# A decoder layer on one core: u and hT moved off the 512-byte grid, a third input buffer in the first block, a late h, a norm taken by tokens, and a last block stored in three pieces

## The chip, the cores and the metric

The kernel runs on one core of a Trainium2 chip. Its time is what the device takes for one launch, in microseconds; the median of three runs is 1830.02 us (1829.93 to 1830.12). The profile is one further execution of the same program. The engines are named as in the profile: PE is TensorE (matmuls; PEld are its weight loads), DVE is VectorE, ACT is ScalarE, POOL is GpSimd, SP is the engine that issues most transfers. "Queue" with SP, ACT or POOL means transfers issued by that engine.

## What is computed

One layer on 256 tokens of width 2048, all in float32:

```python
h = x + 0.5 * swiglu(rms_norm(x, g1), w_gate1, w_up1, w_down1)     # 2048 -> 5632 -> 2048
u = rms_norm(h, g_mix)
proj = u @ w_in                       # forgetting attention: q, k, v, gates; window attention: q, k, v
o = concat(rms_norm(fox(...)), rms_norm(window(...)))
h = h + o @ w_out
y = h + 0.5 * swiglu(rms_norm(h, g2), w_gate2, w_up2, w_down2)

def rms_norm(x, g): return x * rsqrt(mean(x * x, axis=-1) + 1e-6) * g
def swiglu(x, wg, wu, wd): return (silu(x @ wg) * (x @ wu)) @ wd
```

## The kernel before

Each weight is read from HBM once, in pieces of 128 rows by 1024 columns of float32 (512 KB; two tiles of K by 512 columns). Every operand of a large matmul is split into a rounded part and the rest (`hi` and `lo`), and a product is three matmuls: hi by hi (L187), hi by lo (L188), lo by hi (L189). The activations are the stationary operand, loaded 128 x 128 at a time; the weights stream past, 512 columns a time (388 in one projection of the mixer).

`weights` (L90 to L102) fetches a piece on SP's queue into `raw`, rounds it on ACT into `whi` (L100) and takes the rest on DVE into `wlo` (L101); there are four buffers of each. `token_major` (L192) runs over pairs of K tiles, here called groups: for each of two K tiles and for each of two halves of the tokens it issues the three matmuls, 12 a group. `split_scaled` (L158) makes the two parts of an activation: ACT scales and rounds (L160), DVE takes the rest (L161). The normed input is held in two halves, `u0` and `u1`, of eight K tiles each; they are made anew for the first feed-forward stage, for the mixer and for the second feed-forward stage, and `u0` also holds the window attention's output before its projection. The activations inside a feed-forward stage are in `hT`, 44 K tiles.

A feed-forward stage is `gate_up` (L224) with 11 blocks of 512 columns, each a gate product and an up product over u, then `down` (L281) with 4 blocks over hT. After the gate product ACT applies silu with the norm's factor (L243), after the up product DVE multiplies (L247), and PE transposes the result into hT two groups into the next block (`into_rows`, L221).

The first block of the first stage is special (`first_block`, L303): u isn't there yet. For each of eight groups it fetches 256 KB of x, transposed, into `xc` (two buffers, L306), fetches the weight in two halves, makes two K tiles of u, and has ACT square `xc` and POOL add the squares up into `ss1` (L166 to L173). After the block it fetches the constants `cst` (the identity for transposes among them), the positions and x itself by tokens into `h` (L318 to L321) on SP's queue, and `rstd_tokens` (L175) sums the squares over partitions by eight one-column matmuls (L180).

The order in which each engine takes its instructions is not that of the text: a planner lays it out ahead of time by its own estimate of durations, within what depends on what, and gives the fetches of `weights` priority. So the fetches of h stand in SP's queue ahead of some of the first block's own pieces, and the first pieces of the up product's weights too. Each engine and each queue then takes its list in order.

At the end, the last block of the second stage's `down` adds both token halves into h on DVE (L258) and stores each of them, 128 x 512, on ACT's queue (L714).

Tiles are placed one after another in each partition. Unused tiles (`pad`, `sppad`, `mpad`) fill up to a place: before, `h`, `u0`, `u1`, all of `raw`, `whi`, `wlo`, both `hT` and the attention's stationary tiles begin at multiples of 512 bytes.

Of the kernel before, what the change touches and what calls it, by code (L numbers as in the profile page):

```python
# [9 lines left out]
F32 = mybir.dt.float32  # L10
F32R = mybir.dt.float32r
I32 = mybir.dt.int32
BF16 = mybir.dt.bfloat16
AF = mybir.ActivationFunctionType
ALU = mybir.AluOpType
AX = mybir.AxisListType

P = 128
D = 2048
SEQ = 256  # L20
NT = SEQ // P
KD = D // P
FF = 5632
KF = FF // P
# [42 lines left out]
def hybrid_layer(ctx: ExitStack, tc: tile.TileContext, a: dict, out: bass.AP):  # L67
    nc = tc.nc

    keep = ctx.enter_context(tc.tile_pool(name="keep", bufs=1))  # L70
# [19 lines left out]
    def weights(src, tiles=None, at=0):  # L90

        tiles = tiles or weight_tiles()
        if src.shape[1] % 512:
            n = src.shape[1] // 2
            raw, hi, lo = (t.rearrange("p (k n) -> p k n", k=2)[:, :, :n] for t in tiles)
            src = src.rearrange("p (k n) -> p k n", k=2)
        else:
            raw, hi, lo = (t[:, at : at + src.shape[1]] for t in tiles)
        nc.sync.dma_start(raw, src)
        nc.scalar.copy(hi, raw)  # L100
        nc.vector.tensor_tensor(out=lo, in0=raw, in1=hi.bitcast(F32), op=ALU.subtract)  # L101
        return tiles[1:]  # L102


    cst = keep.tile([P, C_END], F32, name="cst")
    vec = keep.tile([P, 256], F32, name="vec")
    pos = keep.tile([P, NT], I32, name="pos")
# [3 lines left out]
    h = keep.tile([P, NT, D], F32, name="h")  # L111
# [5 lines left out]
    m_caus = m_fox[:, P:SEQ]  # L117
    nc.scalar.dma_start(vec[:, :V_END], a["vec"])

    def half_u(i):  # L120
        return keep.tile([P, 8, 2, SEQ], F32R, tag="u%d" % i, name="u%d" % i, bufs=1)

# [5 lines left out]
    def tiles_of(t):  # L128
        return lambda k: t[:, k]
# [36 lines left out]
    def add_squares(ssq, src, first):  # L166

        if first:
            nc.scalar.activation(ssq, src, AF.Square)
            return  # L170
        sq = sp.tile([P, 2, SEQ], F32, tag="sqh", name="sqh", bufs=2)
        nc.scalar.activation(sq, src, AF.Square)
        nc.gpsimd.tensor_tensor(out=ssq, in0=ssq, in1=sq, op=ALU.add)  # L173

    def rstd_tokens(ssq, width, tag):  # L175

        pb = small_ps()
        for t in range(NT):
            for i in range(2):
                nc.tensor.matmul(  # L180
                    pb[:, t : t + 1], lhsT=ssq[:, i, t * P : (t + 1) * P], rhs=ones[:, 0:1],
                    start=(i == 0), stop=(i == 1),
                )
        return mean_rsqrt(sp, pb[:, :NT], NT, width, tag)

    def mm3(o, shi, slo, mhi, mlo, start, stop):
        nc.tensor.matmul(o, lhsT=shi, rhs=mhi, start=start, stop=False)  # L187
        nc.tensor.matmul(o, lhsT=shi, rhs=mlo, start=False, stop=False)  # L188
        nc.tensor.matmul(o, lhsT=slo, rhs=mhi, start=False, stop=stop)  # L189


    def token_major(acc, u, nk, src_w, width=512, then=(), early=None):  # L192

        for kg in range(nk // 2):
            if early is not None:
                parts = early(kg)
            else:
                with tc.high_priority():
                    parts = weights(src_w[kg])
            hi, lo = parts  # L200
            for k in range(2):
                kk = kg * 2 + k
                m = slice(k * 512, k * 512 + width)
                for t in range(NT):
                    ts_ = slice(t * P, (t + 1) * P)
                    mm3(
                        acc[t][:, :width], u(kk)[:, 0, ts_], u(kk)[:, 1, ts_], hi[:, m], lo[:, m],
                        start=(kk == 0), stop=(kk == nk - 1),
                    )
            if kg == 1:  # L210
                for f in then:
                    f()
# [40 lines left out]
    def residual(c, acc, scale):  # L253

        cs = slice(c * 512, (c + 1) * 512)
        for t in range(NT):
# [2 lines left out]
                out=h[:, t, cs], in0=acc[t], scalar=sc, in1=h[:, t, cs], op0=ALU.mult, op1=ALU.add  # L259
            )  # L260

    def next_u(u, ssq, gcol, c):

        cs = slice(c * 512, (c + 1) * 512)
        for t in range(NT):
            sq = sp.tile([P, 512], F32, tag="sqh", name="sqh", bufs=2)
            nc.scalar.activation(sq, h[:, t, cs], AF.Square, accum_out=ssq[:, t, c : c + 1])

        def finish(k, v):
            for j in range(2):  # L270
                split_scaled(u(k + j), v[:, j, :], vec[:, gcol + k + j : gcol + k + j + 1])

        return lambda: into_rows(h[:, :, cs], c, finish)

    def rstd_blocks(ssq, tag):

        tot = sp.tile([P, NT], F32, tag=tag + "s", name=tag + "s")
        nc.vector.tensor_reduce(out=tot, in_=ssq, axis=AX.X, op=ALU.add)
        return mean_rsqrt(sp, tot, NT, D, tag)

    def down(hT, w, then, done):  # L281
        for c in range(D // 512):
            acc = acc_pair()
            token_major(acc, tiles_of(hT), KF, w[c], then=then)
            residual(c, acc, 0.5)
            then = done(c)
        return then


    sp = ctx.enter_context(tc.tile_pool(name="sp", bufs=1))  # L290
    sp.tile([P, 392], F32, name="sppad")
    u1 = new_u()
    ss1 = sp.tile([P, 2, SEQ], F32, tag="ss", name="ss1")
    with tc.tile_pool(name="f1", bufs=1) as fp:
        hT = fp.tile([P, KF, 2, SEQ], F32R, name="hT1")

        zero = fp.tile([P, 512], BF16, name="zero")
        nc.vector.memset(zero, 0.0)
        warm = small_ps()
        for i in range(WARM):  # L300
            nc.tensor.matmul(warm, lhsT=zero[:, 0:P], rhs=zero, start=True, stop=True)

        def first_block(g):  # L303
            def early(kg):
                xc = fp.tile([P, 2, SEQ], F32, tag="xc", name="xc", bufs=2)
                nc.sync.dma_start(xc, a["xT"][kg])  # L306
                tiles = weight_tiles()
                for i in range(2):
                    at = i * 512
                    weights(a["wg1"][0][kg][:, at : at + 512], tiles, at)  # L310
                for j in range(2):
                    k = 2 * kg + j
                    split_scaled(u1(k), xc[:, j, :], vec[:, V_G1 + k : V_G1 + k + 1])
                add_squares(ss1, xc, kg == 0)
                return tiles[1:]

            token_major(g, u1, KD, None, early=early)
            nc.sync.dma_start(cst, a["cst"])  # L318
            nc.sync.dma_start(pos, a["pos"])
            for t in range(NT):  # L320
                nc.sync.dma_start(h[:, t, :], a["x"][t])  # L321
            return rstd_tokens(ss1, D, "r1")

        then = gate_up(fp, u1, None, hT, a["wg1"], a["wu1"], first_block)
        um = new_u()
        ssm = sp.tile([P, NT, 4], F32, tag="ssb", name="ssm", bufs=2)
        then = down(hT, a["wd1"], then, lambda c: [next_u(um, ssm, V_GM, c)])
    rm = rstd_blocks(ssm, "rm")


    with tc.tile_pool(name="mix", bufs=1) as mp:
        ap_ = mp
# [35 lines left out]
        for i, q in ((0, Q1B), (1, Q2B)):  # L368
            nc.vector.scalar_tensor_tensor(
                out=red, in0=cnt[:, i, :], scalar=q, in1=red, op0=ALU.mult, op1=ALU.add  # L370
# [5 lines left out]
            out=part[:, 1, :], in0=red, scalar=-1.0, in1=red, op0=ALU.mult, op1=ALU.max  # L376
        )
        nc.vector.tensor_scalar(
            out=part[:, 1, :], in0=part[:, 1, :], scalar1=-1.0, scalar2=float(np.pi / 2), op0=ALU.mult, op1=ALU.add
# [82 lines left out]
        for c in range(4):  # L462
            acc = acc_pair()
            token_major(acc, um, KD, a["ws"][c], SWC, then=then)
            then = []
# [3 lines left out]
        def fox_mm(hf, i):  # L469
# [11 lines left out]
            out=z, in0=prs[:, :, 0:NH], in1=vec[:, V_BF : V_BF + NH].unsqueeze(1).broadcast_to([P, NT, NH]), op=ALU.add  # L481
# [16 lines left out]
        for t in range(NT):  # L498
            for aa in range(2):
                n = nqk // 2  # L500
                sq = ap_.tile([P, n * HD], F32, tag="sq", name="sq")
                nc.scalar.activation(sq, prs[:, t, NH + aa * n * HD : NH + (aa + 1) * n * HD], AF.Square)
                nc.vector.tensor_reduce(
                    out=ssw[:, t, aa * n : (aa + 1) * n], in_=sq.rearrange("p (j e) -> p j e", e=HD),
# [3 lines left out]
        rw = rw.rearrange("p (t j) -> p t j", t=NT)  # L508
        nc.vector.tensor_scalar_mul(rw[:, :, 0:NH], rw[:, :, 0:NH], HD**-0.5)

        ap_.tile([P, 96], F32, name="mpad")

        def unit_tile(shape, dt, name):
            return ap_.tile(shape, dt, tag="aT", name=name, bufs=3)
# [5 lines left out]
        for t in range(NT):  # L520
# [18 lines left out]
            ts_ = slice(t * P, (t + 1) * P)  # L539
            for aa in range(2):  # L540
                qp = ap_.tile([P, 5, P], F32, tag="qp", name="qp", bufs=2)
                for dst, j0, n in ((qp[:, 0:4, :], aa * 8, 8), (qp[:, 4:5, :], NH + 2 * aa, 2)):
                    nc.vector.tensor_tensor(
                        out=dst.rearrange("p g (b e) -> p b g e", b=2),
                        in0=qr[:, j0 : j0 + n, :].rearrange("p (b g) e -> p b g e", b=2),
# [151 lines left out]
        then = []  # L697
        for c in range(D // 512):
            project(0, c, oTf, rx, then)
            then = [next_u(u2, ss2, V_G2, c)]  # L700
# [3 lines left out]

    rm2 = rstd_blocks(ss2, "rm")
    with tc.tile_pool(name="f2", bufs=1) as fp:
        hT = fp.tile([P, KF, 2, SEQ], F32R, name="hT2")
        then = gate_up(fp, u2, rm2, hT, a["wg2"], a["wu2"])
        y = out.rearrange("(t p) d -> p t d", p=P)

        def store(c):
            cs = slice(c * 512, (c + 1) * 512)
            for t in range(NT):
                nc.scalar.dma_start(y[:, t, cs], h[:, t, cs])  # L714
            return []

        down(hT, a["wd2"], then, store)

# [69 lines left out]
```

## Time and profile before

| what | us |
|---|---|
| median of three runs (lowest, highest) | 1830.02 (1829.93, 1830.12) |
| the profiled execution's own time | 1831.65 |
| its span, first to last event | 1829.5 |
| PE busy | 1818.0 |
| DVE busy | 984.1 |
| ACT busy | 844.9 |
| POOL busy | 21.3 |
| first large matmul starts | 5.89 |
| last matmul starts | 1824.95 |

The page also says that 336 MB are read from HBM, 185 GB/s over the span, and that the granted clock of PE is full in every one of its 40 slices. In the rows of groups, the columns are line, engine and operation, output and inputs by name, shapes, count, then busy us, mean ns of one, and the idle time of the engine before them with what ended it. In timelines a row is start, duration, engine, line, operation. In windows the columns are start and end, length, then busy us and count of each engine, granted clock, busy share of the DMA engines, GB/s. A matmul's duration runs from its start to its modelled end; the next one starts long before that, so the pace of PE is the distance of starts.

### The profile page before, as it was taken

What the parts mean: (1) busy time and instruction counts of PE and PEld (TensorE: products, weight loads), DVE (VectorE), ACT (ScalarE), POOL (GpSimd) and SP (SyncE); (2) the same over time, 40 slices, a digit from 0 to 9 for tenths busy, and PEclk for the clock granted to TensorE, in tenths of its full rate; (3) what the DMA queues carried; (4) which work ended last, traced back from release to release, by engine and by line L of the source; (5) the groups of instructions that cost most, each with busy time, mean ns of one, the idle gap of its engine ahead of it and who ended that gap; (6) DMA issues with size and microseconds to landing.
All of it is one profiled execution on the core that took longest, in us unless ns stands there. A gap on an engine that the chain in (4) does not pass through costs nothing.

```text
span 1829.5 us, 21808 instructions
## 1 busy us (share of the span) xinstructions
PE 1818.0 (99%) x8396; PEld 1513.9 (83%) x8396; DVE 984.1 (54%) x1194; ACT 844.9 (46%) x1073; POOL 21.3 (1%) x27
## 2 busy tenths in 40 slices
PE   8999999999999999999999999999999999999999
PEld 6888888888888888998888788888888888888887
DVE  6545454545544544668766665454554545444443
ACT  6444444444434434554767554444444444433332
POOL 2000000000000000000000000000000000000000
PEclk9999999999999999999999999999999999999999
DMA  8555555555555555564344355555555555556663
GB/s 302 194 186 194 186 194 185 194 185 195 186 193 186 192 193 187 168 209 171 125 140 142 135 175 194 186 194 185 194 186 193 184 188 192 188 193 206 207 203 119
DMA packets 100536, 339.79 MB, mean 186 GB/s; under 512 B 10832, under 2 KB 19152, under 8 KB 100176
## 3 DMA queue, kind: packets, MB, share of 16 engines
q1 hardware_dynamic: 99136, 336.19, 53.4%
q10 hardware_dynamic: 1296, 2.21, 0.4%
q8 instruction: 65, 1.06, 0.2%
q14 instruction: 39, 0.32, 0.0%
HBM read 336.27 MB, written 2.10 MB: 185 GB/s over the span
## 4 chain that ended last, share of the span: by engine, by line
PE 98%; DMA 1%; ACT 0%; DVE 0%; issue 0%; ACTq 0%; DVEq 0%
PE acc L187 31%; PE acc L189 31%; PE acc L188 31%; PE sm L221 1%; PE sm L450 1%; DMA raw<-in_wg 1%; PE sc L565 1%; PE sc L636 1%; PE sm L456 1%; DMA xc<-in_xT 0%; PE sm L617 0%; PE sm L457 0%; DMA vec<-in_vec 0%; PE sm L180 0%; PE sm L551 0%; ACT whi L100 0%
## 5 line engine op out<-in xcount | busy, mean ns | idle before, releaser
L101 DVE TENSOR_TENSOR wlo<-raw,whi 128x1024 fp32r<-128x1024 f32 (+2 forms) x648 | 777.2, 1201 | 799.1 <-ACT whi L100 798.3
L100 ACT CAST whi<-raw 128x1024 fp32r<-128x1024 f32 (+2 forms) x648 | 668.5, 1032 | 895.1 <-PE acc L189 878.7
L187 PE MATMUL acc<-whi,u 128*128 128x512 f32 (+1 forms) x1792 | 694.8, 389 | 4.1 <-ACT u L160 3.5
L188 PE MATMUL acc<-wlo,u 128*128 128x512 f32 (+1 forms) x1792 | 692.6, 387 | 0.1
L189 PE MATMUL acc<-whi,u 128*128 128x512 f32 (+1 forms) x1792 | 690.8, 387 | 0.9 <-DVE u L161 0.9
L187 PEld LDWEIGHTS acc<-whi,u 128*128 128x128 f32 x1792 | 336.8, 188 | 70.3 <-ACT u L160 4.4
L189 PEld LDWEIGHTS acc<-whi,u 128*128 128x128 f32 x1792 | 336.4, 188 | 66.5 <-DVE u L161 1.9
L188 PEld LDWEIGHTS acc<-wlo,u 128*128 128x128 f32 x1792 | 336.9, 188 | 64.7 <-DVE wlo L101 0.9
L187 PE MATMUL acc<-whi,hT 128*128 128x512 f32 x704 | 274.3, 390 | 0.0
L189 PE MATMUL acc<-whi,hT 128*128 128x512 f32 x704 | 273.9, 389 | 0.0
L188 PE MATMUL acc<-wlo,hT 128*128 128x512 f32 x704 | 273.9, 389 | 0.0
L189 PEld LDWEIGHTS acc<-whi,hT 128*128 128x128 f32 x704 | 132.2, 188 | 27.6
L188 PEld LDWEIGHTS acc<-wlo,hT 128*128 128x128 f32 x704 | 132.2, 188 | 27.2
L187 PEld LDWEIGHTS acc<-whi,hT 128*128 128x128 f32 x704 | 132.2, 188 | 27.1
L428 ACT ACTIVATE s<-s,nm 128x128 f32<-128x128 f32 (+1 forms) x64 | 28.3, 445 | 7.6 <-DVE nm L421 4.6
L230 DVE TENSOR_TENSOR hT<-sm,hT 128x512 fp32r<-128x512 f32 x44 | 28.2, 682 | 0.0
L187 PE MATMUL acc<-whi,oTf 128*128 128x512 f32 x64 | 25.2, 393 | 0.0
L188 PE MATMUL acc<-wlo,oTf 128*128 128x512 f32 x64 | 25.0, 391 | 0.0
L189 PE MATMUL acc<-whi,oTf 128*128 128x512 f32 x64 | 24.9, 389 | 0.0
L229 ACT CAST hT<-sm 128x512 fp32r<-128x512 f32 x44 | 23.5, 585 | 0.0
L221 PEld LDWEIGHTS sm<-cst,s 128*128 128x128 f32 x176 | 20.5, 140 | 2.9
L221 PE MATMUL sm<-cst,s 128*128 128x128 f32 x176 | 22.8, 272 | 0.0
(175 smaller groups left out, 563.5 us busy)
## 6 DMA issues: line engine op xcount, KB each, us to landing
raw<-in_wu SPq DMA_DIRECT2D x176, 512.0 KB, 3.2
raw<-in_wd SPq DMA_DIRECT2D x176, 512.0 KB, 3.2
raw<-in_wg SPq DMA_DIRECT2D x168, 512.0 KB, 3.2
raw<-in_wf SPq DMA_DIRECT2D x48, 512.0 KB, 3.6
raw<-in_wo SPq DMA_DIRECT2D x32, 512.0 KB, 3.5
raw<-in_ws SPq DMA_DIRECT2D x32, 388.0 KB, 3.6
raw<-in_wg SPq DMA_DIRECT2D x16, 256.0 KB, 5.3
xc<-in_xT SPq DMA_DIRECT2D x8, 256.0 KB, 4.8
```

The source lines that it names most:

```text
L100: nc.scalar.copy(hi, raw)
L101: nc.vector.tensor_tensor(out=lo, in0=raw, in1=hi.bitcast(F32), op=ALU.subtract)
L187: nc.tensor.matmul(o, lhsT=shi, rhs=mhi, start=start, stop=False)
L188: nc.tensor.matmul(o, lhsT=shi, rhs=mlo, start=False, stop=False)
L189: nc.tensor.matmul(o, lhsT=slo, rhs=mhi, start=False, stop=stop)
L221: nc.tensor.transpose(bt[:, j * SEQ + t * P : j * SEQ + (t + 1) * P], src[:, t, m], ident)
L229: nc.scalar.copy(hs[:, :, 0, :], v)
L230: nc.vector.tensor_tensor(out=hs[:, :, 1, :], in0=v, in1=hs[:, :, 0, :].bitcast(F32), op=ALU.subtract)
L428: nc.scalar.activation(s[:, j, :], s[:, j, :], AF.Exp, bias=nm[:, i, j : j + 1], accum_out=den[:, i, j : j + 1],)
L450: nc.tensor.transpose(bt[:, j * P : (j + 1) * P], src[:, j, :], ident)
L456: nc.tensor.matmul(bo[rows, c0 : c0 + SEQ], lhsT=vals(0, j), rhs=p0[:, j, :], start=True, stop=False)
L565: nc.tensor.matmul(o_, lhsT=qk[aa][:, j, blk * P : (blk + 1) * P], rhs=qk[aa][:, 4 + half, 0:nk], start=True, stop=True,)
```

## The change

Placing. Unused tiles of 256, 128 and 128 bytes are put before, between and behind `u0` and `u1`, so that `u0` begins 256 and `u1` 384 bytes past a multiple of 512; what follows (`raw`, `whi`, `wlo`) is again on multiples of 512. The filling in the pool `sp` is cut from 1568 to 192 bytes, which with the tiles that go (`ss1` as it was, three small ones of its norm) puts the first `hT` 64 bytes past a multiple of 512; a new tile of 128 bytes puts the second 192 past. `mpad` is cut by 64 bytes, so that the attention's tiles stay where they were against 512.

First block. `xc` gets three buffers. From the third group on the weight piece is fetched, rounded and subtracted whole instead of in two halves. The squares of `xc` and POOL's additions are gone. h, the constants and the positions are fetched on POOL's queue instead of SP's; each half of h first gets one column copied from the 13th K tile of u (`held`), so that its fetch waits for the seventh group, and the constants get a column copied from h, so that their fetch waits for h to have landed. The norm is taken as at the later stages: ACT squares h by blocks of 512 columns and sums them along the row (`squares`, 8 instructions with an accumulator each), DVE reduces the four sums (`rstd_blocks`). The eight one-column matmuls are gone.

End. In the last block the last group runs all six matmuls of the first token half, then all six of the second. The first half is evicted and stored whole, the second in two pieces of 256 columns; the stores go by SP's queue.

```diff
+    keep.tile([P, 64], F32, name="upad0")
+    keep.tile([P, 8, 2, SEQ], F32R, tag="u0", name="u0", bufs=1)
+    keep.tile([P, 32], F32, name="upad1")
+    keep.tile([P, 8, 2, SEQ], F32R, tag="u1", name="u1", bufs=1)
+    keep.tile([P, 32], F32, name="upad2")
...
-            for k in range(2):
+            order = [(k, t) for k in range(2) for t in range(NT)]
+            if apart and kg == nk // 2 - 1:
+                order.sort(key=lambda kt: kt[1])
+            for k, t in order:
...
+    def squares(ssq, c):
+        for t in range(NT):
+            sq = sp.tile([P, 512], F32, tag="sqh", name="sqh", bufs=2)
+            nc.scalar.activation(sq, h[:, t, c * 512 : (c + 1) * 512], AF.Square, accum_out=ssq[:, t, c : c + 1])
...
+            if last:
+                for t, a0, n in ((0, 0, 512), (1, 0, 256), (1, 256, 256)):
+                    cs = slice(c * 512 + a0, c * 512 + a0 + n)
+                    nc.vector.scalar_tensor_tensor(
+                        out=h[:, t, cs], in0=acc[t][:, a0 : a0 + n], scalar=0.5, in1=h[:, t, cs],
+                        op0=ALU.mult, op1=ALU.add,
+                    )
+                    nc.sync.dma_start(out[:, t, cs], h[:, t, cs])
+                return []
...
-    sp.tile([P, 392], F32, name="sppad")
+    sp.tile([P, 48], F32, name="sppad")
...
-                xc = fp.tile([P, 2, SEQ], F32, tag="xc", name="xc", bufs=2)
+                xc = fp.tile([P, 2, SEQ], F32, tag="xc", name="xc", bufs=3)
                 nc.sync.dma_start(xc, a["xT"][kg])
                 tiles = weight_tiles()
-                for i in range(2):
-                    at = i * 512
-                    weights(a["wg1"][0][kg][:, at : at + 512], tiles, at)
+                if kg < 2:
+                    for at in (0, 512):
+                        weights(a["wg1"][0][kg][:, at : at + 512], tiles, at)
+                else:
+                    weights(a["wg1"][0][kg], tiles)
...
-                add_squares(ss1, xc, kg == 0)
...
-            nc.sync.dma_start(cst, a["cst"])
-            nc.sync.dma_start(pos, a["pos"])
+            held = u1(12)[:, 1, 0:1].bitcast(F32)
             for t in range(NT):
-                nc.sync.dma_start(h[:, t, :], a["x"][t])
-            return rstd_tokens(ss1, D, "r1")
+                nc.vector.tensor_copy(h[:, t, 0:1], held)
+                nc.gpsimd.dma_start(h[:, t, :], a["x"][t])
+            nc.vector.tensor_copy(cst[:, 0:1], h[:, 1, 0:1])
+            nc.gpsimd.dma_start(cst, a["cst"])
+            nc.gpsimd.dma_start(pos, a["pos"])
+            ss1 = sp.tile([P, NT, 4], F32, tag="ssb", name="ss1", bufs=2)
+            for c in range(4):
+                squares(ss1, c)
+            return rstd_blocks(ss1, "rm")
...
-        ap_.tile([P, 96], F32, name="mpad")
+        ap_.tile([P, 80], F32, name="mpad")
...
+        fp.tile([P, 32], F32, name="fpad")
...
-        down(hT, a["wd2"], then, store)
+        down(hT, a["wd2"], then, store, out=y)
```

More of the change, by code (lines that the diff above doesn't have):

```diff
@@ L189, in mm3, with token_major @@
         nc.tensor.matmul(o, lhsT=slo, rhs=mhi, start=False, stop=stop)
-    def token_major(acc, u, nk, src_w, width=512, then=(), early=None):
+    def token_major(acc, u, nk, src_w, width=512, then=(), early=None, apart=False):
         for kg in range(nk // 2):
@@ L200, in token_major @@
             hi, lo = parts
-            for k in range(2):
+            order = [(k, t) for k in range(2) for t in range(NT)]
+            if apart and kg == nk // 2 - 1:
+                order.sort(key=lambda kt: kt[1])
+            for k, t in order:
                 kk = kg * 2 + k
                 m = slice(k * 512, k * 512 + width)
[L204 to L209, printed above, removed]
+                ts_ = slice(t * P, (t + 1) * P)
+                mm3(
+                    acc[t][:, :width], u(kk)[:, 0, ts_], u(kk)[:, 1, ts_], hi[:, m], lo[:, m],
+                    start=(kk == 0), stop=(kk == nk - 1),
+                )
             if kg == 1:
@@ L260, in residual @@
             )
+    def squares(ssq, c):
+        for t in range(NT):
+            sq = sp.tile([P, 512], F32, tag="sqh", name="sqh", bufs=2)
+            nc.scalar.activation(sq, h[:, t, c * 512 : (c + 1) * 512], AF.Square, accum_out=ssq[:, t, c : c + 1])
     def next_u(u, ssq, gcol, c):
         cs = slice(c * 512, (c + 1) * 512)
-        for t in range(NT):
-            sq = sp.tile([P, 512], F32, tag="sqh", name="sqh", bufs=2)
-            nc.scalar.activation(sq, h[:, t, cs], AF.Square, accum_out=ssq[:, t, c : c + 1])
+        squares(ssq, c)
         def finish(k, v):
@@ L279, in rstd_blocks, with down @@
         return mean_rsqrt(sp, tot, NT, D, tag)
-    def down(hT, w, then, done):
+    def down(hT, w, then, done, out=None):
         for c in range(D // 512):
             acc = acc_pair()
-            token_major(acc, tiles_of(hT), KF, w[c], then=then)
+            last = out is not None and c == D // 512 - 1
+            token_major(acc, tiles_of(hT), KF, w[c], then=then, apart=last)
+            if last:
[4 more added lines that the diff above has]
+                        op0=ALU.mult, op1=ALU.add,
+                    )
+                    nc.sync.dma_start(out[:, t, cs], h[:, t, cs])
+                return []
             residual(c, acc, 0.5)
@@ L290, in hybrid_layer @@
     sp = ctx.enter_context(tc.tile_pool(name="sp", bufs=1))
-    sp.tile([P, 392], F32, name="sppad")
+    sp.tile([P, 48], F32, name="sppad")
     u1 = new_u()
-    ss1 = sp.tile([P, 2, SEQ], F32, tag="ss", name="ss1")
     with tc.tile_pool(name="f1", bufs=1) as fp:
```

## The prediction

> **What bounds the kernel now.** I read the page first (busy times, then the chain that ended last), then the groups with shapes kept apart, then the timeline of PE.
>
> ```profile
> span 1829.5 us, 21808 instructions
> ...
> PE 1818.0 (99%) x8396; PEld 1513.9 (83%) x8396; DVE 984.1 (54%) x1194; ACT 844.9 (46%) x1073; POOL 21.3 (1%) x27
> ...
> PE 98%; DMA 1%; ACT 0%; DVE 0%; issue 0%; ACTq 0%; DVEq 0%
> ```
> ```profile
> L187 PE MATMUL acc<-whi,u 128*128 128x512 f32 x1664 | 651.4, 392 | 4.1 <-ACT u L160 3.5 <-ACT whi L100 0.6
> ...
> L187 PE MATMUL acc<-whi,hT 128*128 128x512 f32 x704 | 274.3, 390 | 0.0
> ...
> L187 PE MATMUL acc<-whi,u 128*128 128x388 f32 x128 | 43.4, 339 | 0.0
> ```
> ```profile
> 1600.10 0.39 PE L187 MATMUL acc<-whi,hT 128*128 128x512 f32 x1
> ...
> 1619.82 0.39 PE L187 MATMUL acc<-whi,hT 128*128 128x512 f32 x1
> ```
> The reader is to see that PE is the chain, and that its price is a spacing, not the 0.39 us of one matmul: matmuls overlap, and from 1600.10 to 1619.82 are 87 starts, 226.7 ns each. Each of L187 to L189 runs as often, so u carries 3 x 1664 = 4992 wide matmuls and 3 x 128 = 384 narrow ones, hT 3 x 704 = 2112. One nanosecond of spacing is worth 5.0 us on u and 2.1 us on hT. Everything else that can be won lies at the two ends of the span.
>
> **The offsets.** Before, u, hT, raw, whi and wlo all begin at multiples of 512 bytes; after, the weight loads of PE read u and hT from 256, 384, 64 and 192 past one, while the streamed whi and wlo stay. The trace has no wide matmul with another offset, so I bound the spacing from both sides.
>
> ```profile
> 26.00:28.00 2.00, 2.00 (x5) 1.61 (x6) 1.11 (x4) 1.65 (x3) 1.19 (x1) 0.50 1.02 412
> ```
> ```profile
> 26.39 0.63 PE L188 MATMUL acc<-wlo,u 128*128 128x512 f32 x1
> 26.82 0.63 PE L187 MATMUL acc<-whi,u 128*128 128x512 f32 x1
> ```
> ```profile
> 7.18 0.40 PE L188 MATMUL acc<-wlo,u 128*128 128x512 f32 x1
> 7.42 0.39 PE L189 MATMUL acc<-whi,u 128*128 128x512 f32 x1
> ...
> 788.99 0.34 PE L187 MATMUL acc<-whi,u 128*128 128x388 f32 x1
> 789.17 0.33 PE L188 MATMUL acc<-wlo,u 128*128 128x388 f32 x1
> 789.34 0.34 PE L189 MATMUL acc<-whi,u 128*128 128x388 f32 x1
> ...
> 791.81 0.34 PE L188 MATMUL acc<-wlo,u 128*128 128x388 f32 x1
> ```
> The first row is a window: PE, PEld, DVE, ACT and POOL busy, granted clock 0.50, DMA share, GB/s. At that clock the same matmul comes every 0.43 us, half of which is 215 ns. At full clock it takes 226.7: some 12 ns per matmul don't come from the array's clock, so something feeds it late. That is the most the offsets can win: 7104 wide matmuls x 12 ns = 85 us. The other end is the spacing just after a stall, up to 240 ns (7.18 to 7.42) before it settles: +13 x 7104 = 92 us. So the extra time depends on how two streams stand to each other, and an address may matter. How finely? In units of one column (215 / 512 = 0.42 ns) the settled wide matmul takes 540, and sixteen narrow ones from 788.99 to 791.81 take 176 ns each, alternating 0.17 and 0.18: about 840 columns a pair. Both are near multiples of 16 columns (34 and 53 of them), which is 64 bytes of f32. If the pattern repeats every 64 bytes, offsets that are all multiples of 64 leave it as it is. This is thin, yet it is the nearest row, and I take the offsets at 0 in the forecast.
>
> [...]
>
> **The first block.** The time stands before the first transposes:
>
> ```profile
> L188 PE MATMUL acc<-wlo,u 128*128 128x512 f32 x38 | 15.4, 409 | 0.1
> L187 PE MATMUL acc<-whi,u 128*128 128x512 f32 x38 | 14.7, 416 | 4.1 <-ACT u L160 3.5 <-ACT whi L100 0.6
> L189 PE MATMUL acc<-whi,u 128*128 128x512 f32 x37 | 13.5, 410 | 0.9 <-DVE u L161 0.9
> L161 DVE SCALAR_TENSOR_TENSOR u<-xc,vec,u 128x256 fp32r<-128x256 f32 x16 | 11.2, 738 | 4.8 <-ACT u L160 4.8
> L101 DVE TENSOR_TENSOR wlo<-raw,whi 128x512 fp32r<-128x512 f32 x16 | 10.8, 727 | 3.3 <-ACT whi L100 3.3
> ...
> L100 ACT CAST whi<-raw 128x512 fp32r<-128x512 f32 x16 | 9.4, 615 | 5.4 <-DMA raw<-in_wg 5.2
> ...
> L160 ACT ACTIVATE u<-xc,vec 128x256 fp32r<-128x256 f32 x16 | 7.2, 499 | 2.0 <-DMA xc<-in_xT 2.0
> ...
> L172 ACT ACTIVATE sqh<-xc 128x512 f32<-128x512 f32 x7 | 4.3, 617 | 0.0
> ```
> ```profile
> 5.89 0.73 PE L187 MATMUL acc<-whi,u 128*128 128x512 f32 x2 [0.61 <-ACT whi L100]
> ...
> 39.30 0.95 PE L180 MATMUL sm<-cst,ss 128*128 128x1 f32 x8
> ```
> The groups are of 0 to 40 us: 113 wide matmuls. From 5.89 to 39.30 pass 33.4 us; 113 x 0.2267 = 25.6 leave 7.8 us of waits (the largest ended by ACT's u, 3.5 us) and of slowed clock after them. Why:
>
> ```profile
> 13.97 1.52 SPq L321 DMA_DIRECT2D h<-in_x  x2
> ...
> 21.81 0.33 SPq L306 DMA_DIRECT2D xc<-in_xT  x1
> ```
> ```profile
> 16.98 8.23 DMA xc<-in_xT
> ```
> ```profile
> 22.00:24.00 2.00, 0.54 (x3) 0.10 (x1) 0.00 (x0) 0.00 (x0) 0.00 (x0) 1.00 1.05 407
> ```
> In the chain (middle fence) the sixth xc, issued at 16.98, lands 8.2 us later, behind 2 MB of h at 407 GB/s; with two xc buffers the next goes out at 21.81 only. After, h, cst and pos leave SP for POOL's queue and wait for the seventh group's u (the copies of `held`), and a third xc lets the transfers run ahead. Without them the first block needs 8 x 768 KB, 6.3 MB: 16 us at 407 GB/s, against 96 x 0.2267 = 21.8 us of PE. Per group of 12 matmuls (2.72 us) ACT had 2 x 0.50 + 2 x 0.62 + 0.62 = 2.9 us and now has 2.2 or less; DVE had 2 x 0.74 + 2 x 0.73 = 2.9, and without POOL's adds beside it nearer the 0.48 that L161 takes elsewhere (row below): 2.4. Both fall under PE's pace. I leave 1.3 us of ramp and take **-6.5 us** (from -3, if the first groups stay tight or h still crowds the last weights, to -7.5). The eight L180 matmuls go (0.95, the last part of it under the next matmul): **-0.8**. The first square no longer stands ahead of the first u on ACT (0.6 us, partly under a transfer): **-0.3** (0 to -0.5).
>
> **What is moved behind.** Eight squares of h, three small copies and the reduction come once h has landed:
>
> ```profile
> L267 ACT ACTIVATE sqh<-h 128x512 f32<-128x512 f32 x16 | 10.0, 623 | 0.0
> ...
> L267 ACT ACTIVATION_READ_ACCUMULATOR sqh<-h 128x1 f32 x16 | 3.0, 185 | 0.0
> ```
> ```profile
> ACT whi L100 <- PE acc L189: 878.7, 554, 2.8
> ```
> ```profile
> h<-in_x SPq DMA_DIRECT2D x2, 1024.0 KB, 7.5
> ```
> ```profile
> 57.83 1.40 DVE L247 SCALAR_TENSOR_TENSOR s<-acc,r1y,s 128x512 f32<-128x512 f32 x2
> ...
> 63.57 1.03 PE L221 MATMUL sm<-cst,s 128*128 128x128 f32 x8
> ```
> 8 x 0.81 = 6.5 us of ACT, in the up block, where ACT's casts wait for PE to free a buffer (878.7 us in all): four whi buffers keep three groups, 8 us, in hand. POOL's queue carries no transfer before, so h's landing is bounded by SP's: 7.5 us under load, and twice that if the two follow each other. Issued at 16 to 20 us, when the seventh group is prepared, it lands at 24 to 35. Squares, norm (the 4.7 us that L137 to L153 took) and silu with its table take some 14 us, and L247, at 57.83 now, would come at about 50: h by 36 costs nothing, and PE's transposes follow only 5.7 us behind L247. I take **0**. A DVE copy into cst and ACT's squares wait for h, with wlo and whi queued behind them; that costs from the point where the wait outlasts those three groups.
>
> **The end.**
>
> ```profile
> 1824.70 1.37 DVE L258 SCALAR_TENSOR_TENSOR h<-acc,h 128x512 f32<-128x512 f32 x2 [7.89 <-PE acc L189]
> ...
> 1825.42 1.02 ACTq L714 DMA_DIRECT2D out<-h  x2
> ```
> ```profile
> L161 DVE SCALAR_TENSOR_TENSOR u<-sm,vec,u 128x256 fp32r<-128x256 f32 x32 | 14.0, 478 | 1.1 <-ACT u L160 1.1
> ```
> The last group goes token half by token half, so the first half is evicted and stored under six matmuls; after the last come two evictions of 256 columns (2 x 0.48, against 1.37) and a store of half the size (128 KB less at 407 GB/s: 0.3). **-0.7** (-0.3 to -0.9).
>
> Sum: -6.5 - 0.8 - 0.3 - 0.7 = -8.3 us. The profiled execution took 1831.65 (span 1829.5 and 2.15 around it) and would take 1823.35; it lies 1.6 above the median, so 1830.02 - 8.3 = **1821.7 us**, own range 1819.5 to 1826 (another order of instructions in the mixer may add or take 1 us).
>
> **Rivals.** (1) The offsets speed PE up: two streams that begin at the same place get out of each other's way. One step of 16 columns, 6.7 ns, on u and hT is 47 us: 1774; on half of them 1798. For it: the 12 ns that half clock hides; against it: the multiples of 16. (2) The offsets slow PE down, the other side: the load of 512 bytes now crosses a multiple of 512 each time, and the matmul stream waits a step. On hT alone +14 us: 1836; on u's two halves +33: 1855; on all 1869. It decides from 8.3 us / 7488 matmuls = 1.1 ns each. For it: spacings up to 240 when the phase is off; against: these settle by themselves to 226.7. (3) Late h: h lands so late that DVE's copy or ACT's squares hold wlo and whi beyond the 8 us in hand, and the stall removed at 22 us comes back in the up block: with 5 to 9 us of it, 1827 to 1831. For it: the sixth xc took 8.2 us under load, and the order is laid out ahead of time; against: h now has its own queue. [...]
>
> **How the numbers follow.** Forecast 0.50, rival 1 0.22, rival 2 0.20, rival 3 0.08. No change means within 0.2%, 1826.4 to 1833.7, about what a measurement of this kernel can tell. Faster: 0.49 + 0.22 + 0.02 = 0.73 (the last from small shares of rivals 2 and 3); same 0.06; slower 0.21. For 8 in 10 the range needs the forecast, rival 3, the milder half of rival 1 (to 1790) and of rival 2 (to 1840).
>
> **What would show it.** Spacing: start to start of the wide matmuls in the two feed-forward stages, 226.7 ns in all four offset cases, or not. First block: no wait above 1 us between the first matmul and the first transposes, and these at about 55.5 instead of 63.57; h on POOL's queue. End: last matmul to the span's end, 4.6 us now, under 4. I am wrong if spacing moved by more than 1 ns, or if a wait on h stands in the up block.

## The result, and the profile after

The changed kernel takes 1847.47 us (median of four, 1847.42 to 1847.53) against 1830.07 us before (1829.93 to 1830.22): 17.4 us more, a ratio of 1.0094 with an interval of 1.0080 to 1.0109. The forecast was 1821.7, inside a range of 1790 to 1840. The second rival, that the offsets slow PE down, is what happened, with another cause than the one it named.

The page and the groups of the kernel after:

```profile
span 1845.6 us, 21776 instructions
...
PE 1838.3 (100%) x8388; PEld 1515.4 (82%) x8388; DVE 978.9 (53%) x1193; ACT 842.8 (46%) x1075; POOL 14.1 (1%) x24
```
```profile
L194 PE MATMUL acc<-whi,u 128*128 128x512 f32 x1664 | 654.4, 395 | 1.0 <-ACT whi L100 1.0
...
L194 PE MATMUL acc<-whi,hT 128*128 128x512 f32 x704 | 278.3, 395 | 0.0
```

The span is 16.1 us longer, and PE is busy for 20 us more with the same wide matmuls: the same 704 over hT now count 278.3 us where they were 274.3. So the loss isn't a wait. The distance of starts shows it. Timeline of PE after: the first two rows bound 47 steps over `u1`, the next two 47 over `u0`, then come 135 over the first `hT` and 300 over the second.

```profile
1205.61 0.40 PE L194 MATMUL acc<-whi,u 128*128 128x512 f32 x1
...
1216.54 0.40 PE L196 MATMUL acc<-whi,u 128*128 128x512 f32 x1
1216.77 0.39 PE L194 MATMUL acc<-whi,u 128*128 128x512 f32 x1
...
1227.43 0.40 PE L196 MATMUL acc<-whi,u 128*128 128x512 f32 x1
```
```profile
599.94 0.40 PE L196 MATMUL acc<-whi,hT 128*128 128x512 f32 x1
...
631.44 0.40 PE L196 MATMUL acc<-whi,hT 128*128 128x512 f32 x1
...
1700.15 0.39 PE L195 MATMUL acc<-wlo,hT 128*128 128x512 f32 x1
...
1768.81 0.39 PE L195 MATMUL acc<-wlo,hT 128*128 128x512 f32 x1
```

They give 232.5 ns for `u1` (384 past a multiple of 512), 226.8 for `u0` (256 past), 233.3 for the first `hT` (64) and 228.9 for the second (192), where before all stood at 226.7. `u0` carries 2592 wide matmuls, `u1` 2400, each hT 1056: 2400 x 5.8 + 1056 x 6.6 + 1056 x 2.2 = 13.9 + 7.0 + 2.3 = 23.2 us, and almost nothing on `u0`. That is more than the whole loss; the start gave some back. PE at the start, and at the first transposes:

```profile
6.64 0.73 PE L194 MATMUL acc<-whi,u 128*128 128x512 f32 x2 [1.00 <-ACT whi L100]
...
56.65 1.03 PE L230 MATMUL sm<-cst,s 128*128 128x128 f32 x8
```

The transposes that stood at 63.57 stand at 56.65, 6.9 us sooner, although the first large matmul starts 0.75 us later than the 5.89 of before. The end:

```profile
1841.14 0.40 PE L196 MATMUL acc<-whi,hT 128*128 128x512 f32 x1
1841.57 0.76 DVE L302 SCALAR_TENSOR_TENSOR h<-acc,h 128x256 f32<-128x256 f32 x2 [0.69 <-PE acc L196]
```

From the last matmul's start to the end of the span pass 4.5 us; before it was 4.55. So the 16.1 us are, to within half a microsecond, 23.2 of spacing, less 6.9 at the start and 0.1 at the end. (Some 0.5 us of `u1`'s spacing fall before those transposes and are counted in both; `u0`'s own 0.1 to 0.2 ns make up for most of it.)

### The profile page after: what moved, and what is told of

The parts are those of the page before. It is cut to its first block, busy times and chain, and to the rows that moved or that the text cites. A ratio compares the mean times of both kernels' runs of the same rounds, so it can differ in the third digit from the quotient of the medians.

```text
span 1845.6 us, 21776 instructions
## 1 busy us (share of the span) xinstructions
PE 1838.3 (100%) x8388; PEld 1515.4 (82%) x8388; DVE 978.9 (53%) x1193; ACT 842.8 (46%) x1075; POOL 14.1 (1%) x24
## 4 chain that ended last, share of the span: by engine, by line
PE 99%; ACT 0%; DMA 0%; DVE 0%; DVEq 0%; issue 0%; ACTq 0%
PE acc L194 32%; PE acc L196 32%; PE acc L195 32%; PE sm L230 1%; PE sm L480 1%; PE sc L595 1%; PE sc L666 1%; PE sm L486 1%; PE sm L647 0%; PE sm L487 0%; DMA xc<-in_xT 0%; PE sm L581 0%; PE sm L187 0%; ACT whi L100 0%; ACT L167 0%; ACT u L167 0%
## 5 line engine op out<-in xcount | busy, mean ns | idle before, releaser
L194 PE MATMUL acc<-whi,u 128*128 128x512 f32 (+1 forms) x1792 | 698.0, 391 | 1.0 <-ACT whi L100 1.0
L194 PEld LDWEIGHTS acc<-whi,u 128*128 128x128 f32 x1792 | 337.1, 188 | 70.2 <-ACT whi L100 1.9
L194 PE MATMUL acc<-whi,hT 128*128 128x512 f32 x704 | 278.3, 395 | 0.0
L196 PE MATMUL acc<-whi,hT 128*128 128x512 f32 x704 | 277.2, 394 | 0.0
L194 PEld LDWEIGHTS acc<-whi,hT 128*128 128x128 f32 x704 | 132.5, 188 | 28.8
L252 ACT ACTIVATE s<-acc,rmy 128x512 f32<-128x512 f32 x44 | 30.0, 684 | 20.8 <-PE acc L196 20.8
L256 DVE SCALAR_TENSOR_TENSOR s<-acc,rmy,s 128x512 f32<-128x512 f32 x44 | 30.9, 743 | 0.8 <-ACT s L252 0.8
L194 PE MATMUL acc<-whi,oTf 128*128 128x512 f32 x64 | 25.2, 394 | 0.0
## 6 DMA issues: line engine op xcount, KB each, us to landing
h<-in_x POOLq DMA_DIRECT2D x2, 1024.0 KB, 10.5
```

What stands on the lines that cost most here:

```text
L252: nc.scalar.activation(s[:, t, :], g[t], AF.Silu, scale=rm[:, t : t + 1])
L256: nc.vector.scalar_tensor_tensor(out=s[:, t, :], in0=up[t], scalar=rm[:, t : t + 1], in1=s[:, t, :], op0=ALU.mult, op1=ALU.mult)
```

## The experiments

Each kernel starts from the changed one. "Offsets at 0" means that `u0`, `u1` and both `hT` begin at multiples of 512 bytes, like `whi` and `wlo`. Spacings are means, from start to start, over all neighbouring wide matmuls that load from the same tile; steps of 250 ns and more, in which a wait, a slowed clock or another matmul stands, are left out (about 25 of 2400 on `u1`, under 100 of 2600 on `u0`). Diffs show the main lines of an edit; the other fillings are resized so that the tiles not named keep their places.

**Offsets back to 0.**

```diff
-    keep.tile([P, 64], F32, name="upad0")
-    keep.tile([P, 32], F32, name="upad1")
-    keep.tile([P, 32], F32, name="upad2")
-    sp.tile([P, 48], F32, name="sppad")
+    sp.tile([P, 32], F32, name="sppad", bufs=1)
-        ap_.tile([P, 80], F32, name="mpad")
+        ap_.tile([P, 96], F32, name="mpad", bufs=1)
-        fp.tile([P, 32], F32, name="fpad")
```

> The changed kernel with u0, u1 and both hT back at multiples of 512 bytes; the first block and the end stay as changed. If the offsets alone made it slower, every wide matmul is back at 226.7 ns (u1 was 232.5, the first hT 233.3, the second 228.9) and the time is near 1847.5 - 24 = 1823. If something else in the change costs time (the new order of instructions, the end), the spacing goes back but the time stays above 1830.

Timeline of PE, 48 steps, the last 42 of them over `u1`, the tile that had moved to 232.5, and the groups over hT (L191 is the line of L194 here):

```profile
1211.05 0.39 PE L193 MATMUL acc<-whi,u 128*128 128x512 f32 x1
...
1221.93 0.39 PE L193 MATMUL acc<-whi,u 128*128 128x512 f32 x1
```
```profile
L191 PE MATMUL acc<-whi,hT 128*128 128x512 f32 x704 | 274.3, 390 | 0.0
```

48 steps in 10.88 us are 226.7 ns, and hT is back at its old 274.3. Both halves of u and both hT are within 0.3 ns of 226.7. The span is 1822.0, which is 23.6 under the changed kernel's 1845.6; the 23.2 summed above from three tiles lie 0.4 from it. The median is 1825.29 us (seven runs, 1823.6 to 1825.4) against 1830.55 on the same chip, ratio 0.9967 (0.9956 to 0.9979). The offsets are the whole loss, and everything else in the change together is a gain.

**Four other offsets:** `u0` 128, `u1` 320, first hT 256, second 448.

```diff
-    keep.tile([P, 64], F32, name="upad0")
+    keep.tile([P, 32], F32, name="upad0", bufs=1)
-    keep.tile([P, 32], F32, name="upad1")
+    keep.tile([P, 48], F32, name="upad1", bufs=1)
...
-    sp.tile([P, 48], F32, name="sppad")
+    sp.tile([P, 96], F32, name="sppad", bufs=1)
...
-        fp.tile([P, 32], F32, name="fpad")
+        fp.tile([P, 48], F32, name="fpad", bufs=1)
...
```

> The changed kernel with u0 at 128, u1 at 320, the first hT at 256, the second at 448. Theory of a pattern that repeats every 256 bytes (0 and 256 both gave 227): u0 like 384 (232.5), u1 like 64 (233.3), first hT 226.7, second hT like 192 (228.9); time near 1848. Rival, each stage has its own cost whatever the offset (hT is hurt because it is hT): first hT at 256 stays above 230. Rival, a load that crosses a multiple of 512 costs a step: already against it that u0 at 256 crosses one and stayed at 227; by it all four are slow here.

Measured: 232.4, 233.3, 226.7 and 229.0 ns, as the theory of 256 bytes has them to 0.1 ns, and the first hT was cured by 256 although it crosses a multiple of 512 at every load. Timeline of PE, 157 steps over it:

```profile
600.09 0.39 PE L195 MATMUL acc<-wlo,hT 128*128 128x512 f32 x1
...
635.67 0.39 PE L196 MATMUL acc<-whi,hT 128*128 128x512 f32 x1
```

The time is 1857.04; my 1848 was added wrongly, since 2592 x 5.7 + 2400 x 6.6 + 1056 x 2.3 = 33 us on 1823 is 1856. So the price follows the offset modulo 256, and not the tile or the stage.

**Everything moved together by 64.**

```diff
-    keep.tile([P, 64], F32, name="upad0")
+    keep.tile([P, 16], F32, name="upad0", bufs=1)
...
-    keep.tile([P, 32], F32, name="upad2")
+    keep.tile([P, 112], F32, name="upad2", bufs=1)
+    wp.tile([P, 1024], F32, tag="raw", name="raw", bufs=4)
+    wp.tile([P, 16], F32, name="wpad", bufs=1)
...
```

> Everything PE reads in the wide matmuls is moved by 64 bytes: u0, u1, both hT, whi and wlo all begin 64 past a multiple of 512. If only the distance between the weight load and the stream counts, it is 0 again: 226.7 ns everywhere, time near 1823. If the weight load's own place on the grid counts, 233 ns on u and hT: 1823 + 7104 x 6.6 ns = 1870.

Timeline of PE, 99 matmuls over the first hT, at 64 past the grid like the stream:

```profile
600.15 0.39 PE L196 MATMUL acc<-wlo,hT 128*128 128x512 f32 x1
...
622.59 0.39 PE L196 MATMUL acc<-wlo,hT 128*128 128x512 f32 x1
```

226.7 ns, as if nothing had moved; u has 226.8 to 227.0. The time is 1825.84. The same hT at the same place costs 233.3 when the stream stays at 0. One stationary tile was not moved here, the attention's `oTf`: over it the spacing is 229.05 ns, where it is 227.08 with the stream at 0, so it pays for a distance of -64, the same as 192. What counts is the distance between the two, not where either lies.

**Only the stream moved by 64.**

```diff
...
+    wp.tile([P, 1024], F32, tag="raw", name="raw", bufs=4)
+    wp.tile([P, 16], F32, name="wpad", bufs=1)
...
```

> Only whi and wlo are moved, to 64 past a multiple of 512; u and hT at 0. If the distance counts, it is -64, the same as 192: 228.9 ns everywhere, 1823 + 7104 x 2.2 ns = 1839. If the weight load's own place counts, 226.7 and 1823. If the stream's own place counts, some third value.

Timeline of PE, 126 matmuls over the first hT:

```profile
599.98 0.39 PE L195 MATMUL acc<-whi,hT 128*128 128x512 f32 x1
...
628.82 0.40 PE L195 MATMUL acc<-whi,hT 128*128 128x512 f32 x1
```

228.9 ns here and 228.9 to 229.1 in all tiles: the price of a distance of 192, with the weight loads at 0. The time is 1841.19 against 1839 expected. With this the theory is settled as far as it goes: weight address minus stream address, modulo 256 bytes.

**The distances between:** 32, 96, 160 and 224, then two runs with the odd multiples of 16 (the tiles made 512 bytes longer and used from inside). The first of these three edits, and the second for u:

```diff
-    keep.tile([P, 64], F32, name="upad0")
+    keep.tile([P, 8], F32, name="upad0", bufs=1)
-    keep.tile([P, 32], F32, name="upad1")
+    keep.tile([P, 16], F32, name="upad1", bufs=1)
...
```
```diff
...
-        return keep.tile([P, 8, 2, SEQ], F32R, tag="u%d" % i, name="u%d" % i, bufs=1)
+        u = keep.tile([P, 4224], F32R, tag="u%d" % i, name="u%d" % i, bufs=1)
+        at = (4, 60)[i]
+        return u[:, at : at + 4096].rearrange("p (k s t) -> p k s t", k=8, s=2)
...
```

> The changed kernel with u0 at 32, u1 at 96, the first hT at 160, the second at 224, whi and wlo at 0: the distances between the ones measured. So far 0, 64, 128, 192 give 226.7, 233.3, 232.4, 228.9 ns. If the pattern is one smooth rise and fall over 256 bytes, 32 gives 229 to 231, 96 about 233, 160 about 231, 224 about 227.5, and 0 is its floor. If the pattern is finer than 64 bytes (the rival that the prediction leaned on), these repeat each other or one of them falls under 226.7.

> Distances that are no multiples of 32: u0 16, u1 240, first hT 48, second hT 208, all else as with offsets at 0. Steps of 32 gave, from 0 on: 226.7, 233.1, 233.3, 234.3, 232.4, 233.4, 228.9, 233.3 ns. If 0 is the only place where the matmuls settle, all four lie at 229 to 235. If the low spacings belong to a neighbourhood of 0 and of 192, 16 and 240 lie under 231 and 208 near 229. Anything under 226.7 would be a gain over the kernel before.

> The other four steps of 16 bytes: u0 80, u1 112, first hT 144, second hT 176. As for the run before: 229 to 235 if only 0 settles; 176 near 229 if 192 has a neighbourhood; under 226.7 would be a gain.

| distance, bytes | 0 | 16 | 32 | 48 | 64 | 80 | 96 | 112 |
|---|---|---|---|---|---|---|---|---|
| ns | 226.7 | 230.8 | 233.1 | 233.3 | 233.3 | 232.1 | 234.3 | 233.3 |

| distance, bytes | 128 | 144 | 160 | 176 | 192 | 208 | 224 | 240 |
|---|---|---|---|---|---|---|---|---|
| ns | 232.4 | 233.3 | 233.4 | 230.0 | 228.9 | 233.3 | 233.3 | 227.7 |

The three runs took 1872.94, 1850.54 and 1861.42 us. My smooth curve falls: 224 is 233.3, not 227.5. There is a floor at 0 with narrow flanks (16 and 240), a shallow one at 192 with a flank at 176 and none at 208, and a plateau everywhere else. Eight of the sixteen lie at 233.1 to 233.4, which is 6.6 ns over the floor. None lies under it: of the distances tried, the kernel before had the best one for matmuls of 512 columns.

The 384 matmuls of 388 columns, all over u in the mixer, don't follow this. With all tiles at 0 they come every 176.6 ns. In the run with four other offsets, PE has 47 steps over `u0` (128) between the first two rows and 47 over `u1` (320, a distance of 64 modulo 256) between the last two:

```profile
769.93 0.34 PE L194 MATMUL acc<-whi,u 128*128 128x388 f32 x1
...
778.08 0.34 PE L196 MATMUL acc<-whi,u 128*128 128x388 f32 x1
778.26 0.34 PE L194 MATMUL acc<-whi,u 128*128 128x388 f32 x1
...
786.72 0.34 PE L196 MATMUL acc<-whi,u 128*128 128x388 f32 x1
```

That is 173.3 and 180.0 ns; `u0` at 80 has 173.3 too. So for these 0 is not the best place. Nor is a period of 256 bytes shown for them: `u1` at 384, in the changed kernel, has 177.8, where `u0` at 128 has 173.3.

**Half a weight load.**

```diff
-        nc.tensor.matmul(o, lhsT=shi, rhs=mlo, start=False, stop=False)
-        nc.tensor.matmul(o, lhsT=slo, rhs=mhi, start=False, stop=stop)
+        nc.tensor.matmul(o[0:64], lhsT=slo[:, 0:64], rhs=mhi, start=False, stop=False)
+        nc.tensor.matmul(o, lhsT=shi, rhs=mlo, start=False, stop=stop)
...
```

> What the load has to do with it. Of the three matmuls of a product the second is now lo by hi with 64 columns of weights instead of 128 (half of that matmul's output rows are left out), the order is hi-hi, lo-hi, hi-lo; u0 at 0, u1 at 64, the first hT at 0, the second at 128. The matmul under which the narrow load runs is the first of the three. If the 12 ns above the array's own pace come from the load reading beside the stream, its spacing falls by about half of that at distance 0 (to 220 or 221) and by half of the excess at 64 and 128; if they are a fixed price of changing weights, it stays at 226.7 at distance 0.

Neither. A load takes 0.19 us and begins with the matmul ahead of its own (299.90 and 299.89 us in the kernel before). Over the first hT at distance 0 the matmul under which the narrow load runs takes 228.9 ns, and the other two, with nothing changed under them, 230.0 and 230.5; single steps range from 224 to 236. At distance 128 all three lie between 231.5 and 234.3. The time is 1855.50 us. With one load of three shorter the even rhythm was gone for all of them, which cost more than it could save. The edit also puts the lo load between the two hi loads, so it isn't shown which of the two did it. What the 12 ns are by which 226.7 stands above half the spacing at the slowed clock, the run leaves open.

**Two xc buffers again,** with offsets at 0.

```diff
-                xc = fp.tile([P, 2, SEQ], F32, tag="xc", name="xc", bufs=3)
+                xc = fp.tile([P, 2, SEQ], F32, tag="xc", name="xc", bufs=2)
```

> All offsets at 0, the first block as changed but with two xc buffers again. With three, the first transposes of the up block came at 56.9 us and no wait above 0.2 us stood in the first block (before: 63.6 us and 7.8 us of waits). If the third buffer is what counts, most of the 7 us come back; if moving h away from the first block's transfers is, under 1 us.

**h, cst and pos on SP's queue again,** with offsets at 0 and three buffers.

```diff
-            held = u1(12)[:, 1, 0:1].bitcast(F32)
             for t in range(NT):
-                nc.vector.tensor_copy(h[:, t, 0:1], held)
-                nc.gpsimd.dma_start(h[:, t, :], a["x"][t])
-            nc.vector.tensor_copy(cst[:, 0:1], h[:, 1, 0:1])
-            nc.gpsimd.dma_start(cst, a["cst"])
-            nc.gpsimd.dma_start(pos, a["pos"])
+                nc.sync.dma_start(h[:, t, :], a["x"][t])
+            nc.sync.dma_start(cst, a["cst"])
+            nc.sync.dma_start(pos, a["pos"])
```

> All offsets at 0, three xc buffers, the norm by tokens, but h, cst and pos on SP's queue again, with no held copies. If moving h away counts, the wait near 22 us returns (3 us or more) and the first transposes come at 60 or later; if the buffer counts, they stay at 57.

PE, the first transposes of the three kernels, each from its own timeline: offsets at 0 alone, then two buffers, then h on SP.

```profile
56.10 1.03 PE L227 MATMUL sm<-cst,s 128*128 128x128 f32 x8
```
```profile
57.98 0.49 PE L227 MATMUL sm<-cst,s 128*128 128x128 f32 x3
```
```profile
61.27 0.49 PE L227 MATMUL sm<-cst,s 128*128 128x128 f32 x3
```

And PE in the kernel with h on SP:

```profile
24.25 1.22 PE L191 MATMUL acc<-whi,u 128*128 128x512 f32 x2 [2.05 <-ACT u L164]
```

The third buffer is worth 1.9 us, between the two sizes expected. (The 56.9 in that expectation stands in no row: it is 56.65 in the changed kernel and 56.10 with offsets at 0.) With h on SP the transposes come 5.2 us later. The old wait near 22 us is back, 2.05 us long and not the 3 expected, with eight matmuls behind it at a granted clock of 0.52. But 1.3 of the 5.2 us are there by the 16th matmul: its first matmuls come 427 ns apart, the same as those at the slowed clock, though the profile's clock row says 1.00 there. The kernel with everything moved together begins in the same way, and is 1.25 us late from there on, with h on POOL's queue. That leaves 3.9 us for moving h. h goes out at 8.06 us here, at 13.97 before and at 21.19 in the changed kernel, so the later start and the other queue aren't told apart; nor were the whole pieces and the missing squares tried alone. The times, one run each, are 1825.69 and 1828.60.

**The table earlier and the old end,** with offsets at 0. In the changed kernel ACT's table load, 1.28 us, stands behind the wait for x; before, it ran ahead of that wait, with the square's line. Timeline of ACT before, then after:

```profile
1.18 1.28 ACT L169 ACT_TABLE_LOAD   x1 [1.18 <-PEq L780]
3.90 0.63 ACT L169 ACTIVATE ss<-xc 128x512 f32<-128x512 f32 x1 [1.44 <-DMA xc<-in_xT]
```
```profile
3.88 1.28 ACT L167 ACT_TABLE_LOAD   x1 [3.88 <-DMA xc<-in_xT]
5.17 0.91 ACT L167 ACTIVATE u<-xc,vec 128x256 fp32r<-128x256 f32 x2
```

```diff
         nc.vector.memset(zero, 0.0)
+        junk = fp.tile([P, 8], F32, name="junk")
+        nc.scalar.mul(junk[:, 0:1], zero[:, 0:1], 1.0)
...
-        down(hT, a["wd2"], then, store, out=y)
+        down(hT, a["wd2"], then, store)
```

> The version that the runs point to: all offsets at 0, the first block as changed, one tiny multiply on ACT ahead of the transfers so that ACT's table is loaded before x lands (as changed, the load of 1.28 us stands behind that wait and the first large matmul starts at 6.7 instead of 5.9), and the old end with two stores on ACT's queue. If the table is what delays the start, the first large matmul starts at 5.4 to 5.9 and the first transposes about 1 us sooner than with offsets at 0 alone (56.1). From the last matmul's start to the end of the span were 4.5 us as changed and 4.6 before: if the three pieces bring nothing, 4.5 to 4.7 here. Time against the kernel before: -7 to -9 us.

Timeline of PE:

```profile
5.60 1.22 PE L191 MATMUL acc<-whi,u 128*128 128x512 f32 x2
...
9.53 0.73 PE L191 MATMUL acc<-whi,u 128*128 128x512 f32 x2 [0.21 <-ACT whi L100]
...
56.84 0.60 PE L227 MATMUL sm<-cst,s 128*128 128x128 f32 x4
```

The first large matmul comes at 5.60 instead of 6.7, so the table was what held it. But it meets data that are not there yet and waits again (0.2 us for `whi`, 0.3 for `wlo`), some of the first steps take 427 ns and more, and the transposes come at 56.84, not sooner than 56.10. The median is 1823.76 us (five runs, 1823.61 to 1824.97) against 1831.02, ratio 0.9961 (0.9947 to 0.9975). That can't be told from the kernel with offsets at 0 alone. From the last matmul to the end of the span are 4.8 us, a little over what I expected, so the end in three pieces isn't shown to be worth more than 0.3. Both versions beat the kernel before and the changed one.

## Why the prediction was wrong

**What bounds the kernel:** right. PE's spacing sets the time, at 5.0 us per ns on u and 2.1 on hT, and the result is just such a change of spacing.

**The offsets** are the step that failed. I took them at 0 because the settled spacings looked like multiples of 16 columns, 64 bytes, and all offsets are multiples of 64. The term that I put at 0 measured +23.2 us. The pattern repeats every 256 bytes: 64, 192 and 384 cost 6.6, 2.2 and 5.8 ns, and only 256 costs next to nothing. From the length of a period in time I had read off a period in address, and the trace held no evidence for that step. The bounds were sound (-12 to +13 ns; measured 0 to +6.6 in the changed kernel, +7.6 at most), and so was the size of one step, 6.7 ns, which the plateau shows (the other distances cost from 1.0 to 7.6 ns). Rival 2 had the sign and the step, at a chance of 0.20, and its sum for all stages, 1869, is near the 1872.9 of the run in which all four tiles stood on the plateau. Its mechanism, a load that crosses a multiple of 512, is refuted: `u0` at 256 crosses at each load and keeps 226.8, and all tiles at 64 together cross and keep 226.7. Rival 1 was refuted for the wide matmuls at every distance tried; the narrow ones gain 3.2 ns at 128 and at 80, some 0.6 us for the half of them that reads `u0`.

**The first block:** right in mechanism, with one wrong term. With offsets at 0, the 7.8 us of waits and slowed clock shrank to 0.4 us, three long steps after the first matmul, so 7.4 were won where I took 6.5; the 0.8 of the eight matmuls went. I gave the earlier start -0.3 and it became +0.84 (+0.75 in the changed kernel): the removed square had carried the table load, which without it moved behind the wait for x. Sum -7.5 (63.57 to 56.10) against -7.6. That the sums meet so closely is luck: two errors of about 1 us cancel, and a start like that of the kernel with everything moved together is 1.25 us longer.

**What is moved behind:** right. h took 10.5 us by POOL's queue and landed at about 30 and 34, inside my 24 to 35; L256 of the changed kernel, which was L247, came at 51.64 against "about 50", and no wait of PE followed. The waits of the kernel after show who did wait:

```profile
ACT sqh L274 <- DMA h<-in_x: 4.6, 2, 2.7
```

ACT stood for 4.6 us in front of its squares, with casts queued behind, and the three groups in hand covered it. Rival 3 had the right place and did not decide.

**The end:** wrong, -0.7 against -0.1. I counted 1.37 us of eviction behind the last matmul; the row shows it beginning at 1824.70, before the last matmul's start at 1824.95, so the first half was already hidden. Two pieces of 256 columns take 0.76 us, more than one of 512 (0.69).

Without the offsets the forecast of -8.3 us stands against -7.5 by the spans (1829.5 and 1822.0) and -5.3 by medians on one chip; the ratio's interval allows -3.8 to -8.1. A span is of one execution, and executions of one kernel spread by as much as these figures differ: the seven with offsets at 0 took 1823.60 to 1823.77 or 1825.29 to 1825.40, and the profiled one is of the shorter ones.

## What to carry to other kernels

Where PE bounds a kernel, print the distance from start to start of its matmuls, tile by tile: here 1 ns of it on u was 5.0 us, and with all that was lost PE's busy share went only from 99% to 100%. For matmuls of 512 float32r columns with weights of 128 x 128, place both tiles at the same offset modulo 256 bytes (226.7 ns here, 227.7 to 234.3 at the other multiples of 16), and check the spacing after anything in front of them grows or shrinks; for another width, try the offsets, since at 388 columns another place was better (173.3 ns at 128, 176.6 at 0). And before a stretch is counted as won, look whether its row begins before the work that it is said to follow (here 1824.70 against 1824.95); when an instruction is removed, look what was riding on it (here a table load of 1.28 us).

## What the runs showed of the hardware that was not expected

The pace of a matmul of 512 float32r columns depends, in these runs, on the address of the weight loads minus that of the stream, modulo 256 bytes: 226.7 ns at 0, 227.7 at 240, 228.9 at 192, 230.0 at 176, 230.8 at 16, and 232.1 to 234.3 at the other eleven multiples of 16. Moving both by 64 bytes changes nothing (226.7 over the first hT). At a granted clock of 0.50 these matmuls come 426 to 427 ns apart (five steps from 26.39 to 28.52 in the kernel before; the same in the kernel with h on SP, behind its wait). Half of that, 213.3 ns or 0.417 a column, is an estimate of what 512 columns take at full clock; by it the 226.7 are 544 columns and the plateau's 233.3 are 560, one step of 16 more. At 388 columns the order is another: 176.6 ns at 0 and 173.3 at 128. With one load in three shorter, and placed between the other two, the spacings at distance 0 rose to 228.9 to 230.5. Why 256 bytes, and what the 13 ns are (12 by the rounded 0.43 of the prediction) that remain at distance 0 over half the spacing at that clock, is open; no run here separated the loads from the streams.
